# Feed-forward gates in pairs of weight tiles, by seven products of quarters

## The chip, the cores and the metric

The kernel runs on one core of one Trainium2 chip. The time is device microseconds of one execution. The engines are named as in the profile: PE (TensorE, matrix products; PEld is its weight load), DVE (VectorE), ACT (ScalarE), POOL (GpSimd) and SP (SyncE, which issues the DMAs).

## What is computed

One encoder layer on 512 tokens of width 1024: a half-step feed-forward, a mixing stage (gated linear attention and a short convolution), cross-attention to a memory of 256 tokens, a second half-step feed-forward, and a last norm. The change touches the two feed-forwards alone:

```python
def rms_norm(x, g):
    xf = x.astype(jnp.float32)
    y = xf * lax.rsqrt(jnp.mean(xf * xf, axis=-1, keepdims=True) + EPS)
    return (y * g.astype(jnp.float32)).astype(x.dtype)

def swiglu(h, w_gate, w_up, w_down):
    return (jax.nn.silu(h @ w_gate) * (h @ w_up)) @ w_down

x = x + 0.5 * swiglu(rms_norm(x, ffn1_norm[l]), ffn1_w_gate[l], ffn1_w_up[l], ffn1_w_down[l])
...
x = x + 0.5 * swiglu(rms_norm(x, ffn2_norm[l]), ffn2_w_gate[l], ffn2_w_up[l], ffn2_w_down[l])
```

All inputs are fp32; the inner width is 2816.

## The kernel before

Everything lies transposed: 128 channels on the partitions, T = 512 tokens along the free axis. The width 1024 is KD = 8 tiles of 128 rows, the inner width KF = 22 tiles. An fp32 product is made of three products of a reduced type (fp32r): each operand is split into a high part, rounded, and a low part, the rest, and `mm3` (L76 to L79) adds high by high, high by low of x, and low by high. A tile of 128 output channels over the whole width is a "unit": 8 k-tiles by 3 matmuls of 128x512, 24 matmuls into one bank of PSUM.

`unit` (L57) fetches the weights of one unit, 128x1024, by one DMA on SP's queue into `raw` (4 buffers); ACT makes the high part `whi` and DVE the low part `wlo` (`wsplit`, L70 to L72; 3 buffers each). These three steps get a higher priority than their place in the program (AHEAD = 150), and a scheduler then orders each engine's instructions by priority and by which buffers are free. Every engine works through its list in that order.

`ffn` (L237) is called twice, with the name "a" (L360) and "b" (L970). For each of 22 f it computes a gate unit into `pg` and an up unit into `pu`. `finish` (L241) takes both: DVE multiplies them by `rstd`, the norm's factor per token (L243 and L247, into fa and fb), ACT takes silu (L245, fs), POOL multiplies the two into h (L249, fh), and h is split at once into hh (ACT, L126) and hl (DVE, L127), which lie in the pool `big` (44 tiles of 128x512). The norm's gain is in `xs`, the split x; its factor rstd is not needed for the products, and comes only after f = 2 in "a" and f = 1 in "b" (`norm.tok`, `norm.rows`: two matmuls into sp_n and a copy by ACT, L204). After the 22 tiles come 8 tiles d of the output, each with three units of `wd` (DOWN, L235) over the 22 tiles of h.

Four buffers of temporary kinds matter: fa, fb, fs and fh have two buffers each.

Of the kernel before, what the change touches and what calls it, by code (L numbers as in the profile page):

```python
# [20 lines left out]
KF = DFF // P  # L21
# [5 lines left out]
AHEAD = 150  # L27
# [3 lines left out]
def layer_kernel(ctx: ExitStack, tc: tile.TileContext, t: dict, outT: bass.AP):  # L31
    nc = tc.nc
    const = ctx.enter_context(tc.tile_pool(name="const", bufs=1))
    resid = ctx.enter_context(tc.tile_pool(name="resid", bufs=1))
    wpool = ctx.enter_context(tc.tile_pool(name="wpool", bufs=2))
    act = ctx.enter_context(tc.tile_pool(name="act", bufs=1))
    tmp = ctx.enter_context(tc.tile_pool(name="tmp", bufs=2))
# [74 lines left out]
    for i in range(WARM):  # L112
# [4 lines left out]
    gains = const.tile([P, 6, KD], F32, name="gains")  # L117
# [50 lines left out]
    class Norm:  # L168
# [23 lines left out]
        def add(self, d):  # L192
            self.scale(d)
            self.square(d)
# [12 lines left out]
    def first_units(wgu, norm):  # L207

        g, u = unit(None, D, "ga0"), unit(None, D, "ua0")
        sent = []  # L210
        for k in range(0, KD, 2):
            c = slice(k * P, (k + 2) * P)
            queue = nc.scalar if k == 0 else nc.sync
            for n, w in enumerate((g, u)):
                i = queue.dma_start(w[0][:, c], wgu[0, n][:, c])
                if k > 0:
                    sent.append(i)
            if k == 0:
# [12 lines left out]
        norm.scaled = done[-1]  # L231
        return g[1:], u[1:]


    DOWN = ((0, 8), (8, 15), (15, KF))  # L235

    def ffn(wgu, wd, norm, nxt, name, first=None):  # L237
        hs = []
        rstd = None

        def finish(f, pg, pu):  # L241
            a = tmp.tile([P, T], F32, tag="fa", name=f"fa_{name}{f}")
            nc.vector.tensor_tensor(a, pg, rstd, ALU.mult)  # L243
            s = tmp.tile([P, T], F32, tag="fs", name=f"fs_{name}{f}")
            nc.scalar.activation(s, a, AF.Silu)  # L245
            b = tmp.tile([P, T], F32, tag="fb", name=f"fb_{name}{f}")
            nc.vector.tensor_tensor(b, pu, rstd, ALU.mult)  # L247
            h = tmp.tile([P, T], F32, tag="fh", name=f"fh_{name}{f}")
            nc.gpsimd.tensor_tensor(h, s, b, ALU.mult)  # L249
            hh, hl = big(f"hh_{name}{f}", F32R), big(f"hl_{name}{f}", F32R)  # L250
            split(h, hh, hl)
            hs.append((hh, hl))

        waiting = []
        wait = 1 if first is None else 2
        for f in range(KF):
            pg, pu = bank(f"pg_{name}{f}"), bank(f"pu_{name}{f}")
            if f == 0 and first is not None:
                g, u = first
                for k in range(KD):  # L260
                    mm_cols(pg, g, xs, [(k, k)], k == 0, k == KD - 1)
                    mm_cols(pu, u, xs, [(k, k)], k == 0, k == KD - 1)
                for d in range(KD):
                    norm.square(d, norm.scaled)
            else:
                if f == wait:
                    norm.tok()
                behind = norm.landed if f == 1 and first is not None else None
                mm_cols(pg, unit(wgu[f, 0], D, f"g{name}{f}", behind), xs, ALL)
                flush()  # L270
                mm_cols(pu, unit(wgu[f, 1], D, f"u{name}{f}", behind), xs, ALL)
                if f == wait:
                    rstd = norm.rows()
            waiting.append((f, pg, pu))
            if rstd is not None:
                for w in waiting:
                    finish(*w)
                waiting = []

        for d in range(KD):  # L280
            us = [unit(wd[d, :, k0 * P:k1 * P], (k1 - k0) * P, f"d{name}{d}{k0}") for k0, k1 in DOWN]
            if nxt is None and d == KD - 1:
                finale(us, hs)
                return
            ps = bank(f"pd_{name}{d}")
            for u, (k0, k1) in zip(us, DOWN):
                mm_cols(ps, u, hs, [(k - k0, k) for k in range(k0, k1)], k0 == 0, k1 == KF)
            nc.vector.scalar_tensor_tensor(x[d], ps, 0.5, x[d], ALU.mult, ALU.add)
            (nxt or nf).add(d)
# [151 lines left out]
    rstd = nmix.rows()  # L441
# [526 lines left out]

    nf = Norm(GFIN, "nf")
    ffn(t["w2gu"], t["w2d"], n2, None, "b")  # L970


# [61 lines left out]
```

## Time and profile before

| | us |
|---|---|
| median of 3 runs | 1102.85 (1102.79 to 1102.97) |
| profiled execution | 1102.6 |
| its span, from the first to the last instruction | 1100.8 |
| PE busy | 1093.7 (99%) |
| DVE busy | 548.8 (50%) |
| ACT busy | 380.8 (35%) |
| POOL busy | 137.0 (12%) |

Busy time is the sum of an engine's instructions, overlaps within the engine counted once. Matmuls are pipelined: what one costs is the distance between the starts of two that follow one another, not the duration shown. Names such as pg_a stand for all tiles of that name in the stage a.

### The profile page before, as it was taken

How to read it: one execution, taken by the hardware profiler on the slowest of the kernel's cores; microseconds unless marked ns; L12 is line 12 of the kernel's file. 1: busy time of each engine (PE TensorE's matmuls, PEld its weight loads, DVE VectorE, ACT ScalarE, POOL GpSimd, SP SyncE). 2: the span in 40 equal slices, each digit the busy share in tenths (PEclk: the TensorE clock that was granted, in tenths of full speed). 3: DMA queues.
4: the chain of work that ended last, by engine and by line, in shares of the span. 5: the costliest groups of instructions: out<-in, count | busy, mean ns of one | idle time of the engine just before them, and what ended most of it. 6: DMA issues, size and time to landing. Idle time of an engine off the chain costs nothing.

```text
span 1100.8 us, 13905 instructions
## 1 busy us (share of the span) xinstructions
PE 1093.7 (99%) x5736; PEld 918.7 (83%) x5736; DVE 548.8 (50%) x711; ACT 380.8 (35%) x533; POOL 137.0 (12%) x112
## 2 busy tenths in 40 slices
PE   9999999999999999999999999999999999999997
PEld 8888888888888988889888888888888888888887
DVE  6545454543333479776555365635545454532223
ACT  6332223332322364424343344434222222232321
POOL 0211010100111013101002200222101010101000
PEclk9999999999999999999999999999999999999999
DMA  8232323233334322223353221222322323233312
GB/s 265 81 102 92 112 83 110 92 92 90 105 89 123 124 77 92 86 64 130 112 175 96 96 77 39 81 97 92 96 98 94 100 93 110 78 103 99 92 53 78
DMA packets 35136, 109.15 MB, mean 99 GB/s; under 512 B 4992, under 2 KB 8064, under 8 KB 35072
## 3 DMA queue, kind: packets, MB, share of 16 engines
q1 hardware_dynamic: 34640, 107.97, 31.1%
q8 instruction: 45, 0.74, 0.3%
q10 hardware_dynamic: 432, 0.29, 0.1%
q14 instruction: 19, 0.16, 0.0%
HBM read 106.14 MB, written 2.10 MB: 98 GB/s over the span
## 4 chain that ended last, share of the span: by engine, by line
PE 99%; DVE 0%; DVEq 0%; issue 0%; POOL 0%; POOLq 0%
PE pg_a L77 4%; PE pg_b L77 4%; PE pu_a L77 4%; PE pg_a L78 4%; PE pg_a L79 4%; PE pg_b L79 4%; PE pd_a L78 4%; PE pu_b L79 4%; PE pu_a L78 4%; PE pd_a L77 4%; PE pu_a L79 4%; PE pg_b L78 4%; PE pu_b L78 4%; PE pu_b L77 4%; PE pd_a L79 4%; PE pd_b L78 3%
## 5 line engine op out<-in xcount | busy, mean ns | idle before, releaser
L77 PE MATMUL pg_a<-xh,whi_ga 128*128 128x512 f32 x176 | 69.2, 393 | 0.0
L77 PE MATMUL pg_b<-xh,whi_gb 128*128 128x512 f32 x176 | 68.9, 391 | 0.0
L77 PE MATMUL pu_a<-xh,whi_ua 128*128 128x512 f32 x176 | 68.8, 391 | 0.0
L79 PE MATMUL pg_a<-xh,wlo_ga 128*128 128x512 f32 x176 | 68.6, 390 | 0.0
L78 PE MATMUL pg_a<-xl,whi_ga 128*128 128x512 f32 x176 | 68.5, 389 | 0.0
L78 PE MATMUL pg_b<-xl,whi_gb 128*128 128x512 f32 x176 | 68.5, 389 | 0.0
L79 PE MATMUL pg_b<-xh,wlo_gb 128*128 128x512 f32 x176 | 68.5, 389 | 0.0
L79 PE MATMUL pu_b<-xh,wlo_ub 128*128 128x512 f32 x176 | 68.5, 389 | 0.0
L78 PE MATMUL pu_a<-xl,whi_ua 128*128 128x512 f32 x176 | 68.5, 389 | 0.0
L79 PE MATMUL pd_a<-hh_a,wlo_da 128*128 128x512 f32 x176 | 68.5, 389 | 0.0
L79 PE MATMUL pu_a<-xh,wlo_ua 128*128 128x512 f32 x176 | 68.5, 389 | 0.0
L78 PE MATMUL pu_b<-xl,whi_ub 128*128 128x512 f32 x176 | 68.5, 389 | 0.0
L77 PE MATMUL pu_b<-xh,whi_ub 128*128 128x512 f32 x176 | 68.5, 389 | 0.0
L78 PE MATMUL pd_a<-hl_a,whi_da 128*128 128x512 f32 x176 | 68.5, 389 | 0.0
L77 PE MATMUL pd_a<-hh_a,whi_da 128*128 128x512 f32 x176 | 68.5, 389 | 0.0
L78 PE MATMUL pd_b<-hl_b,whi_db 128*128 128x512 f32 x154 | 59.9, 389 | 0.0
L79 PE MATMUL pd_b<-hh_b,wlo_db 128*128 128x512 f32 x154 | 59.9, 389 | 0.0
L77 PE MATMUL pd_b<-hh_b,whi_db 128*128 128x512 f32 x154 | 59.9, 389 | 0.0
L72 DVE TENSOR_TENSOR wlo_db<-raw_db,whi_db 128x896 fp32r<-128x896 f32 (+1 forms) x24 | 28.4, 1182 | 53.8 <-ACT whi_db L71 53.1
L249 POOL TENSOR_TENSOR fh_a<-fs_a,fb_a 128x512 f32<-128x512 f32 x22 | 31.9, 1452 | 185.3 <-DVE fb_a L247 154.5
L249 POOL TENSOR_TENSOR fh_b<-fs_b,fb_b 128x512 f32<-128x512 f32 x22 | 30.4, 1381 | 197.8 <-DVE fb_b L247 171.5
L72 DVE TENSOR_TENSOR wlo_da<-raw_da,whi_da 128x896 fp32r<-128x896 f32 (+1 forms) x24 | 28.4, 1182 | 49.8 <-ACT whi_da L71 49.1
(351 smaller groups left out, 2651.2 us busy)
## 6 DMA issues: line engine op xcount, KB each, us to landing
raw_gb<-in_w2gu SPq DMA_DIRECT2D x22, 512.0 KB, 3.5
raw_ub<-in_w2gu SPq DMA_DIRECT2D x22, 512.0 KB, 3.4
raw_ga<-in_w1gu SPq DMA_DIRECT2D x21, 512.0 KB, 3.5
raw_ua<-in_w1gu SPq DMA_DIRECT2D x21, 512.0 KB, 3.4
raw_da<-in_w1d SPq DMA_DIRECT2D x16, 448.0 KB, 3.4
raw_db<-in_w2d SPq DMA_DIRECT2D x16, 448.0 KB, 3.3
raw_da<-in_w1d SPq DMA_DIRECT2D x8, 512.0 KB, 3.6
raw_wk<-in_wk SPq DMA_DIRECT2D x8, 512.0 KB, 3.7
```

The lines of the kernel that those rows point to most:

```text
L72: nc.vector.tensor_tensor(lo[:, c], raw[:, c], hi[:, c].bitcast(F32), ALU.subtract))
L77: nc.tensor.matmul(ps, lhsT=whi, rhs=xhi, start=start, stop=False)
L78: nc.tensor.matmul(ps, lhsT=whi, rhs=xlo, start=False, stop=False)
L79: last_mm[0] = nc.tensor.matmul(ps, lhsT=wlo, rhs=xhi, start=False, stop=stop)
L249: nc.gpsimd.tensor_tensor(h, s, b, ALU.mult)
```

## The change

The gate tiles f and f+1 are computed as a pair, for f = 4, 6, ... 18 in "a" and f = 2, 4, ... 18 in "b" (8 and 9 pairs); f = 20 and 21 and the first tiles stay as they were, and so do all up units. The pair is one product of a 2 by 2 block matrix of weights (two tiles by two halves of the width) with a 2 by 2 block matrix of x (two halves of the width by two halves of the tokens). It is done by Strassen's scheme in Winograd's form: seven products of quarters instead of eight, each 4 k-tiles by 3 matmuls of 128x256, 84 matmuls of 256 columns (`seventh`) in place of 48 of 512. Four combinations of the halves of the weights are made in place in the two raw tiles, per pair (`pair_units`): four DVE instructions of 512 columns (L294, L302, L303, L312), and seven 512-column splits on ACT and DVE (L282, L283) into four tiles W0 to W3. Four combinations of the quarters of x are made once per stage (`quarter_sums`, `fill` of k = 0 to 3; L248 to L257), with their splits, into 16 tiles of `big` called t0 to t3. The results are summed up after the products: U is a copy by ACT (L353), the other five sums are DVE instructions of 128x256 that read PSUM (`add`, L350).

The 16 tiles take room in `big`. So h of f below 15 stays one fp32 tile, and is split later, at f = 20 and 21 (`late`).

PE's order in a pair, by the products' names: A (first half, with W0), Dq (W0), nine matmuls of the up unit, B (W1), three of the up unit, A (second half, W1), the rest of the up unit, B (W2), seven of the second up unit, Fq (W2), the rest of it, Dq (W3).

```diff
+    def quarter_sums(gi, name):
+        tiles = [[big(f"t{n}_{name}{k}", F32R) for k in range(KD // 2)] for n in range(4)]
+        def fill(k):
+            b1 = tmp.tile([P, T], F32, tag="fb", name=f"b1_{name}{k}")
+            b2 = tmp.tile([P, T], F32, tag="fs", name=f"b2_{name}{k}")
+            nc.scalar.activation(b1, x[k], AF.Copy, scale=gains[:, gi, k:k + 1])
+            nc.scalar.activation(b2, x[k + 4], AF.Copy, scale=gains[:, gi, k + 4:k + 5])
+            e, l = slice(0, HALF_T), slice(HALF_T, T)
+            ta = tmp.tile([P, T], F32, tag="fa", name=f"ta_{name}{k}")
+            tb = tmp.tile([P, T], F32, tag="fh", name=f"tb_{name}{k}")
+            sums = (tb[:, l], tb[:, e], ta[:, e], ta[:, l])
+            nc.vector.tensor_tensor(sums[2], b1[:, l], b1[:, e], ALU.subtract)
+            nc.vector.tensor_tensor(sums[1], b2[:, l], sums[2], ALU.subtract)
+            nc.vector.tensor_tensor(sums[0], b2[:, l], b1[:, l], ALU.subtract)
+            nc.vector.tensor_tensor(sums[3], b2[:, e], sums[1], ALU.subtract)
+            for n in range(4):
+                split(sums[n], tiles[n][k][:, e], tiles[n][k][:, l])
+        return tiles, fill
...
+        FIRST, LAST = (4 if first is not None else 2), 20
+        KEPT = 15
...
+            def halves(raw, c, hi, lo, at):
+                nc.scalar.activation(hi[:, at], raw[:, c], AF.Copy)
+                nc.vector.tensor_tensor(lo[:, at], raw[:, c], hi[:, at].bitcast(F32), ALU.subtract)
...
+                    halves(a, q0, *w, q0)
+                    nc.vector.tensor_tensor(a[:, q0], a[:, q0], b[:, q0], ALU.subtract)
+                    halves(a, q0, *w, q1)
...
+                    nc.vector.tensor_tensor(b[:, q0], b[:, q0], b[:, q1], ALU.add)
+                    nc.vector.tensor_tensor(a[:, q0], b[:, q1], a[:, q0], ALU.subtract)
+                    halves(a, q0, *w, q0)
+                    halves(a, q1, *w, q1)
...
+                    nc.vector.tensor_tensor(a[:, q1], a[:, q1], a[:, q0], ALU.subtract)
+                    halves(b, q0, *w, q0)
+                    halves(a, q1, *w, q1)
...
+                    halves(b, q1, *w, q0)
...
+        def seventh(ps, w, at, xb, start):
+            for k in range(KD // 2):
+                c = slice(at + k * P, at + (k + 1) * P)
+                for n, (wq, xq) in enumerate(((w[0], xb[k][0]), (w[0], xb[k][1]), (w[1], xb[k][0]))):
+                    nc.tensor.matmul(ps, lhsT=wq[:, c], rhs=xq, start=(start and k == 0 and n == 0),
+                                     stop=(k == KD // 2 - 1 and n == 2), skip_group_check=True)
...
+        def pair(f):
...
+            A, B, Dq, Fq = ab[:, e], ab[:, l], df[:, e], df[:, l]
...
+            U, V, E, C12 = c2[:, l], c2[:, e], c1, c1
...
+            seventh(A, w, 0, xq(0, e), True)
+            nc.scalar.copy(U, A)
+            seventh(Dq, w, T, t3, True)
+            w = units[1]()
+            seventh(B, w, 0, t2, False)
+            add(V, U, B)
+            seventh(A, w, T, xq(4, e), False)
+            mm_cols(pus[0], unit(wgu[f, 1], D, f"u{name}{f}"), xs, ALL)
+            w = units[2]()
+            seventh(B, w, 0, t1, False)
+            add(E, U, B)
+            add(c2[:, l], E, Dq)
+            seventh(Fq, w, T, xq(4, l), False)
+            add(C12, E, Fq)
+            finish(f, ((A, e), (C12, l)), pus[0])
+            mm_cols(pus[1], unit(wgu[f + 1, 1], D, f"u{name}{f + 1}"), xs, ALL)
+            w = units[3]()
+            seventh(Dq, w, 0, t4, False)
+            add(c2[:, e], V, Dq)
+            finish(f + 1, ((c2, slice(0, T)),), pus[1])
...
+            if f < KEPT:
+                h = big(f"h_{name}{f}")
+            else:
+                h = tmp.tile([P, T], F32, tag="fh", name=f"fh_{name}{f}")
...
+            if f < KEPT:
+                late.append(two)
+            else:
+                two()
...
+            if FIRST <= f < LAST:
+                if (f - FIRST) % 2 == 0:
+                    pair(f)
+                continue
...
+            if f >= LAST:
+                for _ in range(len(late) // (KF - f)):
+                    late.pop(0)()
...
+            if f < FIRST and (first is None or f > 0):
+                for _ in range(-(-len(fills) // (FIRST - f))):
+                    fills.pop(0)()
```

How it moves instructions is shown at three places. In the rows, the number behind the stage's letter is f, the last number is the program's own count. On DVE, from the products of tile 4 with rstd on, the order before is:

```order
L243 TENSOR_TENSOR fa_a4_574<-pg_a4_512,rstd_n1_400 128x512
L72 TENSOR_TENSOR wlo_ua5_620<-raw_ua5_618,whi_ua5_619 128x1024
L247 TENSOR_TENSOR fb_a4_578<-pu_a4_513,rstd_n1_400 128x512
L72 TENSOR_TENSOR wlo_ga6_664<-raw_ga6_662,whi_ga6_663 128x1024
L127 TENSOR_TENSOR hl_a4_583<-fh_a4_580,hh_a4_582 128x512
L243 TENSOR_TENSOR fa_a5_648<-pg_a5_586,rstd_n1_400 128x512
L72 TENSOR_TENSOR wlo_ua6_694<-raw_ua6_692,whi_ua6_693 128x1024
```

Each unit's low part stands between two instructions that wait for PE. After the change, from the last product of Fq on (the first row is the later half of tile 4; c1 is C12, the sum that reads Fq, c2 holds U, V and the results of tile 5), DVE has this order; raw_ga6 and raw_ga7 are the tiles a and b of the next pair:

```order
L376 TENSOR_TENSOR fa_a4_723<-c1_a4_588,rstd_n1_452 128x256
L283 TENSOR_TENSOR wlo_g0a6_798<-raw_ga6_793,whi_g0a6_797 128x512
L294 TENSOR_TENSOR raw_ga6_793<-raw_ga6_793,raw_ga7_795 128x512
L302 TENSOR_TENSOR raw_ga7_795<-raw_ga7_795 128x512
L283 TENSOR_TENSOR wlo_g0a6_798<-raw_ga6_793,whi_g0a6_797 128x512
L303 TENSOR_TENSOR raw_ga6_793<-raw_ga7_795,raw_ga6_793 128x512
L380 TENSOR_TENSOR fb_a5_783<-pu_a5_587,rstd_n1_452 128x512
L283 TENSOR_TENSOR wlo_g1a6_830<-raw_ga6_793,whi_g1a6_829 128x512 x2
L312 TENSOR_TENSOR raw_ga6_793<-raw_ga6_793 128x512
L72 TENSOR_TENSOR wlo_ua6_864<-raw_ua6_862,whi_ua6_863 128x1024
L350 TENSOR_TENSOR c2_a4_589<-c2_a4_589,pdf_a4_585 128x256
L376 TENSOR_TENSOR fa_a5_779<-c2_a4_589,rstd_n1_452 128x512
```

The two weight tiles W0 and W1 of the next pair and its first up unit now stand together, between the sum that waits for Fq and the last sum of the pair. On ACT the same stretch before is:

```order
L245 ACTIVATE fs_a4_576<-fa_a4_574 128x512
L71 ACTIVATE whi_ga6_663<-raw_ga6_662 128x1024
L126 ACTIVATE hh_a4_582<-fh_a4_580 128x512
L71 ACTIVATE whi_ua6_693<-raw_ua6_692 128x1024
L245 ACTIVATE fs_a5_650<-fa_a5_648 128x512
```

And after, from silu of tile 4 on:

```order
L378 ACTIVATE fs_a4_726<-fa_a4_723 128x512
L282 ACTIVATE whi_g0a6_797<-raw_ga6_793 128x512
L282 ACTIVATE whi_g1a6_829<-raw_ga6_793 128x512 x2
L71 ACTIVATE whi_ua6_863<-raw_ua6_862 128x1024
L282 ACTIVATE whi_g2a6_892<-raw_ga7_795 128x512
L282 ACTIVATE whi_g2a6_892<-raw_ga6_793 128x512
L378 ACTIVATE fs_a5_781<-fa_a5_779 128x512
L353 COPY c2_a6_792<-pab_a6_787 128x256
```

The copy U of the next pair (last row) stands behind silu of tile 5, which reads fa of tile 5, the last row of DVE's list above. The third place is DVE ahead of the first pair of "a". Before:

```order
L243 TENSOR_TENSOR fa_a3_500<-pg_a3_438,rstd_n1_400 128x512
L72 TENSOR_TENSOR wlo_ua4_546<-raw_ua4_544,whi_ua4_545 128x1024
L127 TENSOR_TENSOR hl_a2_435<-fh_a2_432,hh_a2_434 128x512
L247 TENSOR_TENSOR fb_a3_504<-pu_a3_439,rstd_n1_400 128x512
L72 TENSOR_TENSOR wlo_ga5_590<-raw_ga5_588,whi_ga5_589 128x1024
```

After, from fb of tile 3 on:

```order
L380 TENSOR_TENSOR fb_a3_562<-pu_a3_497,rstd_n1_452 128x512
L72 TENSOR_TENSOR wlo_ua4_661<-raw_ua4_659,whi_ua4_660 128x1024
L127 TENSOR_TENSOR t3_a2_198<-ta_a2_482,t3_a2_198 128x256
L254 TENSOR_TENSOR ta_a3_570<-b1_a3_566 128x256
L256 TENSOR_TENSOR tb_a3_571<-b2_a3_567,b1_a3_566 128x256
L255 TENSOR_TENSOR tb_a3_571<-b2_a3_567,ta_a3_570 128x256
L257 TENSOR_TENSOR ta_a3_570<-b2_a3_567,tb_a3_571 128x256
L127 TENSOR_TENSOR t0_a3_187<-tb_a3_571,t0_a3_187 128x256
L127 TENSOR_TENSOR t1_a3_191<-tb_a3_571,t1_a3_191 128x256
```

The up unit's low part (L72) stands behind the two products of tile 3 and most of the fill of k = 2, and the fill of k = 3 stands behind that.

## Rows read from the trace of the kernel before

**Rows 1.** The page: busy time by engine, granted clock by slice, the chain
```profile
PE 1093.7 (99%) x5736; PEld 918.7 (83%) x5736; DVE 548.8 (50%) x711; ACT 380.8 (35%) x533; POOL 137.0 (12%) x112
...
PEclk9999999999999999999999999999999999999999
...
PE 99%; DVE 0%; DVEq 0%; issue 0%; POOL 0%; POOLq 0%
```

**Rows 2.** PE's timeline: start, duration, line, out<-in, shape; 24 matmuls apart
```profile
61.86 0.39 PE L77 MATMUL pg_a<-xh,whi_ga 128*128 128x512 f32 x1
...
67.30 0.39 PE L77 MATMUL pu_a<-xh,whi_ua 128*128 128x512 f32 x1
```

**Rows 3.** PE's timeline, 256 columns: the first and the fifty-first
```profile
507.00 0.28 PE L77 MATMUL mkps<-mem,whi_wk 128*128 128x256 f32 x1
...
513.00 0.28 PE L79 MATMUL mkps<-mem,wlo_wk 128*128 128x256 f32 x1
```

**Rows 4.** DVE's groups by shape: count | busy us, mean ns | idle before
```profile
L72 DVE TENSOR_TENSOR wlo_ua<-raw_ua,whi_ua 128x1024 fp32r<-128x1024 f32 x21 | 25.7, 1224 | 4.5 <-ACT whi_ua L71 4.5
...
L243 DVE TENSOR_TENSOR fa_a<-pg_a,rstd_n 128x512 f32<-128x512 f32 x22 | 15.2, 690 | 26.5 <-PE pg_a L79 26.5
...
L750 DVE TENSOR_TENSOR mk<-mkps,mk 128x256 fp32r<-128x256 f32 x8 | 3.3, 418 | 0.0
```

**Rows 5.** DVE's timeline: two independent instructions in a row
```profile
43.02 0.68 DVE L243 TENSOR_TENSOR fa_a<-pg_a,rstd_n 128x512 f32<-128x512 f32 x1
43.62 0.68 DVE L247 TENSOR_TENSOR fb_a<-pu_a,rstd_n 128x512 f32<-128x512 f32 x1
```

**Rows 6.** DVE and POOL at three places: timelines of either engine, x counts merged ones
```profile
106.50 2.32 DVE L72 TENSOR_TENSOR wlo_ga<-raw_ga,whi_ga 128x1024 fp32r<-128x1024 f32 x1 [0.23 <-ACT whi_ga L71]
...
106.44 1.29 POOL L249 TENSOR_TENSOR fh_a<-fs_a,fb_a 128x512 f32<-128x512 f32 x1 [9.59 <-DVE fb_a L247]
...
410.05 1.77 DVE L517 TENSOR_TENSOR mn<-k,mn 128x512 f32<-128x512 f32 x1
...
408.99 2.29 POOL L519 TENSOR_TENSOR ta<-k,ta 128x512 f32<-128x512 f32 x1
...
430.54 2.26 DVE L568 SCALAR_TENSOR_TENSOR S<-S,dec,dS 128x128 f32<-128x128 f32 x6
...
430.77 1.29 POOL L709 TENSOR_TENSOR cv<-cv,rstd_nmix 128x512 f32<-128x512 f32 x1 [13.62 <-DVE cv L708]
```

**Rows 7.** ACT's groups by shape: silu
```profile
L245 ACT ACTIVATE fs_a<-fa_a 128x512 f32<-128x512 f32 x22 | 13.5, 616 | 1.7 <-DVE fa_a L243 1.7
```

**Rows 8.** Timelines of ACT and PE in stage a: rstd, and the first matmul of f = 4
```profile
40.56 0.57 ACT L204 COPY rstd_n<-sp_n 128x512 f32<-128x512 f32 x1
...
50.98 0.39 PE L77 MATMUL pg_a<-xh,whi_ga 128*128 128x512 f32 x1
```

**Rows 9.** Stage b: first matmul of f = 2 (PE), table load, DVE's first product, POOL's h
```profile
751.25 0.40 PE L77 MATMUL pg_b<-xh,whi_gb 128*128 128x512 f32 x1
...
752.32 1.28 ACT L245 ACT_TABLE_LOAD   x1
...
753.00 0.68 DVE L243 TENSOR_TENSOR fa_b<-pg_b,rstd_n 128x512 f32<-128x512 f32 x1
...
754.43 2.54 POOL L249 TENSOR_TENSOR fh_b<-fs_b,fb_b 128x512 f32<-128x512 f32 x2 [10.47 <-ACT fs_b L245]
```

**Rows 10.** DMA issues: out<-in, queue, count, KB each, median us to landing
```profile
raw_ga<-in_w1gu SPq DMA_DIRECT2D x21, 512.0 KB, 3.5
```

More of the change, by code (lines that the diff above doesn't have):

```diff
@@ L235, in layer_kernel @@
     DOWN = ((0, 8), (8, 15), (15, KF))
+    HALF_T = T // 2
+    def quarter_sums(gi, name):
[16 more added lines that the diff above has]
+        return tiles, fill
@@ L237, in ffn, with pair_units, tiles, first_two @@
     def ffn(wgu, wd, norm, nxt, name, first=None):
-        hs = []
+        hs = [None] * KF
         rstd = None
+        FIRST, LAST = (4 if first is not None else 2), 20
+        KEPT = 15
+        tq, fill = quarter_sums(norm.gi, name)
+        late = []
+        def pair_units(f):
+            q0, q1 = slice(0, T), slice(T, D)
+            raws = []
+            def tiles(n, m):
+                return (wpool.tile([P, m], F32R, tag="whi", name=f"whi_g{n}{name}{f}", bufs=3),
+                        wpool.tile([P, m], F32R, tag="wlo", name=f"wlo_g{n}{name}{f}", bufs=3))
+            def halves(raw, c, hi, lo, at):
+                nc.scalar.activation(hi[:, at], raw[:, c], AF.Copy)
+                nc.vector.tensor_tensor(lo[:, at], raw[:, c], hi[:, at].bitcast(F32), ALU.subtract)
+            def first_two():
+                with tc.high_priority(AHEAD):
+                    for i in range(2):
+                        raw = wpool.tile([P, D], F32, tag="raw", name=f"raw_g{name}{f + i}", bufs=4)
+                        nc.sync.dma_start(raw, wgu[f + i, 0])
+                        raws.append(raw)
+                    a, b = raws
+                    w = tiles(0, D)
+                    halves(a, q0, *w, q0)
+                    nc.vector.tensor_tensor(a[:, q0], a[:, q0], b[:, q0], ALU.subtract)
+                    halves(a, q0, *w, q1)
+                return w
+            def next_two():
+                with tc.high_priority(AHEAD):
+                    a, b = raws
+                    w = tiles(1, D)
+                    nc.vector.tensor_tensor(b[:, q0], b[:, q0], b[:, q1], ALU.add)
+                    nc.vector.tensor_tensor(a[:, q0], b[:, q1], a[:, q0], ALU.subtract)
+                    halves(a, q0, *w, q0)
+                    halves(a, q1, *w, q1)
+                return w
+            def third_two():
+                with tc.high_priority(AHEAD):
+                    a, b = raws
+                    w = tiles(2, D)
+                    nc.vector.tensor_tensor(a[:, q1], a[:, q1], a[:, q0], ALU.subtract)
+                    halves(b, q0, *w, q0)
+                    halves(a, q1, *w, q1)
+                return w
+            def final_one():
+                with tc.high_priority(AHEAD):
+                    a, b = raws
+                    w = tiles(3, D)
+                    halves(b, q1, *w, q0)
+                return w
+            return first_two, next_two, third_two, final_one
@@ new lines, in seventh, with xq @@
+        def seventh(ps, w, at, xb, start):
[4 more added lines that the diff above has]
+                                     stop=(k == KD // 2 - 1 and n == 2), skip_group_check=True)
+                tick()
+        def pair(f):
+            e, l = slice(0, HALF_T), slice(HALF_T, T)
+            def xq(k0, tok):
+                return [(xs[k0 + k][0][:, tok], xs[k0 + k][1][:, tok]) for k in range(KD // 2)]
+            t3, t2, t1, t4 = [[(q[:, e], q[:, l]) for q in row] for row in tq]
+            units = pair_units(f)
+            ab, df = bank(f"pab_{name}{f}"), bank(f"pdf_{name}{f}")
+            pus = [bank(f"pu_{name}{f + i}") for i in range(2)]
+            A, B, Dq, Fq = ab[:, e], ab[:, l], df[:, e], df[:, l]
+            c1 = tmp.tile([P, T], F32, tag="sq", name=f"c1_{name}{f}", bufs=2)[:, 0:HALF_T]
+            c2 = tmp.tile([P, T], F32, tag="c2", name=f"c2_{name}{f}", bufs=1)
+            U, V, E, C12 = c2[:, l], c2[:, e], c1, c1
+            add = lambda o, a, b: nc.vector.tensor_tensor(o, a, b, ALU.add)
+            w = units[0]()
+            seventh(A, w, 0, xq(0, e), True)
[18 more added lines that the diff above has]
+            finish(f + 1, ((c2, slice(0, T)),), pus[1])
@@ L241, in finish @@
         def finish(f, pg, pu):
             a = tmp.tile([P, T], F32, tag="fa", name=f"fa_{name}{f}")
-            nc.vector.tensor_tensor(a, pg, rstd, ALU.mult)
+            for part, tok in pg:
+                nc.vector.tensor_tensor(a[:, tok], part, rstd[:, tok], ALU.mult)
             s = tmp.tile([P, T], F32, tag="fs", name=f"fs_{name}{f}")
@@ L247, in finish, with two @@
             nc.vector.tensor_tensor(b, pu, rstd, ALU.mult)
-            h = tmp.tile([P, T], F32, tag="fh", name=f"fh_{name}{f}")
+            if f < KEPT:
+                h = big(f"h_{name}{f}")
+            else:
+                h = tmp.tile([P, T], F32, tag="fh", name=f"fh_{name}{f}")
             nc.gpsimd.tensor_tensor(h, s, b, ALU.mult)
-            hh, hl = big(f"hh_{name}{f}", F32R), big(f"hl_{name}{f}", F32R)
-            split(h, hh, hl)
-            hs.append((hh, hl))
+            def two():
+                hs[f] = big(f"hh_{name}{f}", F32R), big(f"hl_{name}{f}", F32R)
+                split(h, *hs[f])
+            if f < KEPT:
+                late.append(two)
+            else:
+                two()
         waiting = []
         wait = 1 if first is None else 2
+        fills = [lambda k=k: fill(k) for k in range(KD // 2)]
         for f in range(KF):
+            if FIRST <= f < LAST:
+                if (f - FIRST) % 2 == 0:
+                    pair(f)
+                continue
             pg, pu = bank(f"pg_{name}{f}"), bank(f"pu_{name}{f}")
@@ L273, in ffn @@
                     rstd = norm.rows()
-            waiting.append((f, pg, pu))
+            if f >= LAST:
+                for _ in range(len(late) // (KF - f)):
+                    late.pop(0)()
+            waiting.append((f, ((pg, slice(0, T)),), pu))
             if rstd is not None:
@@ L278, in ffn @@
                 waiting = []
+            if f < FIRST and (first is None or f > 0):
+                for _ in range(-(-len(fills) // (FIRST - f))):
+                    fills.pop(0)()
+        for two in late:
+            two()
         for d in range(KD):
```

## The prediction

> **What bounds the kernel now.** I read the page's first parts, then PE's timeline, then the other engines in the stretches that the change touches. PE is busy for 1093.7 of 1100.8 us, the chain that ended last is 99% PE and the granted clock reads 9 in every slice, while DVE is busy half of the time and POOL an eighth [rows 1]. So time is lost or won only where PE has fewer columns to stream or has to wait. Two things about PE's price must be seen. A 128x512 matmul occupies its slot for 0.2267 us: the first of a gate unit starts at 61.86 and the first of the next unit, 24 matmuls on, at 67.30 [rows 2]; the 0.39 us in the duration column is the length of one in the pipeline. A 128x256 matmul that changes its weights each time occupies 0.1200 us: fifty of them lie between 507.00 and 513.00 [rows 3]. Half the columns cost 53% of the slot.
>
> **What PE gains.** Two gate units were 48 matmuls of 512 columns: 48 x 0.2267 = 10.88 us. Seven products of 12 matmuls of 256 columns are 84 x 0.1200 = 10.08 us. A pair gains 0.80 us, and 8 pairs in the first stage ("a", f from 4 to 19) and 9 in the second ("b", f from 2) gain 13.6 us if PE never waits. A pair with its two up units then has 20.96 us of PE work against 21.76 before. The gain is thin: it is gone if a 256-column matmul takes 10.88/84 = 129.5 ns.
>
> The Trainium skill ("TensorE: Matmul & The Clock Gate", section "Back-to-back issue gap") gives sustained spacings of 81 ns for 128 and 131 ns for 512 columns, so that few columns are dear; about 98 ns for 256 by a straight line would make seven products 8.2 us against 6.3 and the change a loss of 1.9 us a pair. The trace does not agree: its spacings for this data type are 120 and 226.7 ns [rows 2, 3], and the sum goes by them.
>
> **What DVE gets.** Prices: 1024 columns 1.22, 512 columns 0.69, 256 columns 0.42 us from start to end [rows 4]; an instruction that depends on nothing just before it starts 0.60 us after a 512 one [rows 5]. Per pair of f, DVE had four splits of 1024 (L72), two of 512 (L127) and four products with rstd, some 9 us in 21.76. Now it has two 1024, fourteen 512 and seven 256, about 2 x 1.15 + 14 x 0.65 + 7 x 0.4 = 14 to 15 us in 20.96. That fits in the sum. It does not fit in the order: the sums of PE's results stand in DVE's one queue ahead of the next pair's weights, so DVE can't begin on most of the next weights until the seventh product of this pair but one (Fq) is out.
>
> I set zero at the start of a pair's first product. By PE's order the slots end: A first half 1.44, Dq 2.88, three quarters of a unit of up in pieces around B and A's second half until 11.20, B 12.64, Fq 15.67, second up unit 19.52, Dq 20.96; in the next pair A and Dq again to 23.84, then nine up matmuls to 25.88, then B. B writes the bank that ACT's copy U (L353) reads, so its first matmul waits for U. U stands on ACT behind silu of f+1, which waits for fa of f+1, which stands on DVE behind the whole preparation. The queue from Fq, each end in us: C12 16.30 (a 256-column result in PSUM is readable some 0.2 after its slot), fa's later half 16.73, W0 low part 17.34, a-=b 18.05, then POOL (next paragraph) and b+= 19.77, W0's second low part 20.38, a=b-a 21.09, fb 21.69, two low parts of W1 22.90, a-=a 23.50, the up unit's low part (1024) 24.65, c2's earlier half 24.98, fa 25.69; ACT then has silu (0.62 [rows 7]) to 26.34 and U to 26.61. B could start at 25.88 and starts at 26.66: **0.77 us of waiting per step from pair to pair**, of which the up unit's low part, wanted at 24.29 by its third matmul and ready at 24.65, is already 0.36. One pair then takes about 21.73 us, against 21.76 before: the gain is given back.
>
> **POOL inside that queue.** h of f (L385, two SBUF inputs) is released by its silu near 17.4 and asks while DVE runs a-=b. The trace shows how two such instructions meet: POOL's product alone takes 1.29; started at 106.44, it made DVE's split of 106.50 take 2.32 instead of 1.23; in the stretch at 409 the two engines take turns, POOL's instruction at 408.99 lasting 2.29 and DVE's at 410.05 lasting 1.77 instead of 0.69. DVE instructions that read PSUM are not held: six from 430.54 took 2.26, 0.377 each, while POOL ran from 430.77 [rows 6]. So b+= waits for POOL, about 1.1 us. Lower bound of this term: zero, if POOL is the one that waits; upper: 1.2. I take 1.1, by the rows at 106 and 410. Before, the same collision cost nothing, because PE's next weights were two units ahead.
>
> The Trainium skill ("VectorE: DVE Perf Modes", section "The DRAIN you can't avoid") says that the next DVE instruction does not start until the pipe is empty. Rows at 43.02 and 43.62 show a 0.69 us instruction overlapped by 0.09 [rows 5]; by that rule seven or eight independent instructions of the queue would cost 0.6 us more per pair, some 9 us in all. The trace decides, and the sum has the overlap.
>
> Of 15 steps from pair to pair 13 are of this kind: 13 x 0.77 = 10.0 us. In the other two (16 to 18 in each stage) an h that is not kept is split at once, one more 512 instruction on each of DVE and ACT ahead of the up unit: 0.77 + 0.6 = 1.4 each, 2.8 us. Bounds for a step are 0 (POOL waits) and 1.4.
>
> **Start of the pairs.** The sums of x (fill) of k = 2 and 3 stand behind rstd. In "a" rstd ends at 41.13 and the pair's first product would start at 50.98 [rows 8]. DVE's queue from there holds 15 instructions of 512, seven of 256 and one of 1024 up to the up unit's low part: 9.0 + 2.6 + 1.2 = 12.8 us, and POOL takes two to three turns for h0, h1, h2: it ends near 56.5. The third up matmul wants it at 53.93: 2.6 us. The fill of k = 3 (one low part, four sums, two more low parts and POOL's h3) follows to 59.8, and PE, which has gone on to 58.5, waits 1.3 more: **3.9 us**. In "b" the pair would start at 751.25; rstd is followed by a table load of 1.28 us, and DVE's first product starts at 753.00 [rows 9]. The buffers for the fills come free only after POOL's h0 and h1, which end at 756.97 in the trace [rows 9]; the fill of k = 3 is ready at 763.6 and the next up unit's high part, for which a buffer of W0 must come free, at 764.6, where PE by its own work would be at 761.0: **3.6 us**. Bounds for the two together: 4 (no turns of POOL) and 9.
>
> **What costs nothing.** ACT (U, silu, copies) has some 11 us in a pair. Post-sums V and c2's later half are ready within 0.2 us of need. The same bytes are loaded; b's raw tile is freed at 12.7, and a load lands in 3.5 us [rows 10], at 16.2, 1.1 us before a-=b wants it. Late splits: 15 h of 1.3 us on DVE and ACT, some 20 us, lie in the two plain gate and up units (21.8 us) and the first down unit, whose matmuls want h one after another. If that cover is gone the cost is 1 or 2 us per stage.
>
> **Sum.** -13.6 + 10.0 + 2.8 + 3.9 + 3.6 = +6.7 us, on a profiled execution of 1102.6 us (span 1100.8) beside a median of 1102.85. Forecast 1109.5 us.
>
> **Rivals.**
> - PE stays the bound: POOL waits for DVE's run of back-to-back instructions instead of breaking in, 1.1 us leaves the queue, and a step costs nothing (25.88 against 25.5). Then -13.6 + 2 x 0.3 + 7 = -6: 1097 us, **faster**. For it: POOL's instruction of 408.99 did wait for DVE. Against: it then got its turn. It decides from 0.8 us of queue less per pair.
> - A draw: the collision is half as dear or falls later. A step of 0.4: -13.6 + 6 + 7 = -0.6: 1102 us.
> - A longer queue: every DVE instruction pays its whole duration (0.6 us a step), b's tile lands late, V or c2 is late too: 1.5 per step: -13.6 + 22.5 + 8.5 = +17: 1120 us.
> - The narrow products don't run at 0.120: at 0.1295 the gain is nil and the waits stay small, since PE is slower: about 1110. It moves no end of the range. Against it: fifty in a row at 0.1200 [rows 3].
>
> **How the numbers follow.** About 0.2% (2.2 us) is what a measurement of this kernel can tell from no change. Forecast 0.50 (its own range 1104 to 1116), faster rival 0.25, draw 0.15, longer queue 0.07, narrow products 0.03. Faster by over 0.2%: 0.25 and a fifth of the draw, 0.28. Slower: nearly all of the forecast, the longer queue and the narrow products, 0.56. Within 0.2%: 0.16. Both signs hold much of the chance, so the range runs from 1094 (faster rival with starts of 4 us) to 1118.
>
> **What the profile would show.** Right: in the pairs PE's B waits on ACT's copy of A, 0.5 to 1.1 us each time, the pair takes 21.5 to 22.0 us, a DVE sum on the raw tiles lasts near 1.8 instead of 0.69 beside POOL's h, and PE idles some 4 us soon after each rstd. Wrong: pairs of 20.96 us with no wait, or products at a spacing other than 0.120.

## The result: 17.8 us slower, mainly through queues

| | before | after |
|---|---|---|
| median of 4 runs each, us | 1102.85 | 1120.61 (1120.01 to 1121.47) |
| ratio to before, 95% interval | 1 | 1.0161 (1.0144 to 1.0179) |
| profiled execution's span, us | 1100.8 | 1119.8 |

The direction was forecast, the size was not: +6.7 us was worked out, +17.8 came, and 1120.6 lies above the range (1118). The page of the changed kernel, against [rows 1]: PE's matmuls are busy for 4 us more although they stream fewer columns (busy time counts durations: of the 0.60 us between two starts below, 0.40 count as busy), DVE for 107 us more, and the granted clock's row shows 9 throughout, since a slice of 28 us hides what a few us show.

```profile
PE 1097.4 (98%) x6348; PEld 934.3 (83%) x6348; DVE 656.1 (59%) x1030; ACT 440.4 (39%) x683; POOL 148.7 (13%) x112
...
PEclk9999999999999999999999999999999999999999
```

The time from one pair's first matmul to the next pair's, read from PE's timeline, shows where the 19.0 us between the spans lie. Each pair took 21.76 before (two f), and 84 x 0.1200 + 48 x 0.2267 = 20.96 is PE's work now. One usual step, from PE's timeline:

```profile
99.41 0.28 PE L331 MATMUL pab_a<-xh,whi_g0a 128*128 128x256 f32 x1
...
121.53 0.28 PE L331 MATMUL pab_a<-xh,whi_g0a 128*128 128x256 f32 x1
```

All steps:

| stretch | stage a | stage b |
|---|---|---|
| first pair | 24.89 | 26.46 |
| steps to f = 6 ... 14 (a), 4 ... 14 (b) | 22.05 to 22.12 | 22.27, then 22.09 to 22.11 |
| f = 16 | 22.92 | 22.93 |
| f = 18 (to the first matmul of f = 20) | 23.50 | 23.50 |

Over 20.96, that is 3.9 + 5.5 us in the first pairs, 12.7 in eleven usual steps and 9.0 in four last ones. The pairs of "a" also begin 1.5 late (52.47 for 50.98). With the 13.6 that the columns save: -13.6 + 3.9 + 5.5 + 12.7 + 9.0 + 1.5 = 19.0. The rest of the kernel, the two stretches with the late splits among it, takes what it took (the two plain tiles 21.8 us in either stage).

One usual step as PE's timeline has it (start, duration, line, out<-in, shape; in brackets its idle time just before and what ended it). Two rows that follow one another, 0.23 apart where nothing is in the way:

```profile
102.52 0.40 PE L78 MATMUL pu_a<-xl,whi_ua 128*128 128x512 f32 x1
103.12 0.50 PE L79 MATMUL pu_a<-xh,wlo_ua 128*128 128x512 f32 x1 [0.20 <-DVE wlo_ua L72]
103.46 0.40 PE L77 MATMUL pu_a<-xh,whi_ua 128*128 128x512 f32 x1
...
104.60 0.39 PE L79 MATMUL pu_a<-xh,wlo_ua 128*128 128x512 f32 x1
105.17 0.50 PE L331 MATMUL pab_a<-t_a,whi_g1a 128*128 128x256 f32 x2 [0.17 <-ACT c_a L353]
```

PE stands for 0.60 instead of 0.23 before the up unit's third matmul, the first that needs its low part, and for 0.57 before B, which waits for ACT's copy U: 0.37 and 0.34. Behind each wait the second start is late too: 103.46 lies 0.34 behind 103.12. So the nine up matmuls up to B take 2.88 instead of 2.04, 0.84 more. The queue behind it, in ACT's timeline (silu of f+1, then U) and in DVE's (the tile combinations; the low part of the up unit; fa of f+1), and POOL's product:

```profile
104.22 0.63 ACT L378 ACTIVATE fs_a<-fa_a 128x512 f32<-128x512 f32 x1 [0.65 <-DVE fa_a L376]
104.76 0.35 ACT L353 COPY c_a<-pab_a 128x256 f32<-128x256 f32 x1
```

```profile
95.81 0.69 DVE L294 TENSOR_TENSOR raw_ga<-raw_ga,raw_ga 128x512 f32<-128x512 f32 x1
96.54 1.66 DVE L302 TENSOR_TENSOR raw_ga<-raw_ga 128x512 f32<-128x512 f32 x1
...
101.85 1.22 DVE L72 TENSOR_TENSOR wlo_ua<-raw_ua,whi_ua 128x1024 fp32r<-128x1024 f32 x1
102.99 0.42 DVE L350 TENSOR_TENSOR c_a<-c_a,pdf_a 128x256 f32<-128x256 f32 x1
103.44 0.69 DVE L376 TENSOR_TENSOR fa_a<-c_a,rstd_n 128x512 f32<-128x512 f32 x1
...
95.98 1.67 POOL L385 TENSOR_TENSOR h_a<-fs_a,fb_a 128x512 f32<-128x512 f32 x1 [11.54 <-ACT fs_a L378]
```

POOL's instruction starts at 95.98, while L294 runs, and by its length gets its turn near that one's end; b+= (L302) takes 1.66 instead of 0.69. That is [rows 6] again, with 0.97 us. The Trainium skill, "SBUF — State Buffer", section "SBUF: two separate sides", tells of one pair of ports for DVE and GpSimd, taken whole by a GpSimd instruction or by a DVE instruction with two SBUF inputs, whichever starts first, while the other waits; the 1.66 and the 1.67 here agree.

### The profile page after: what moved, and what is told of

Read it like the earlier page. It is cut to its first block, busy times and chain, and to the rows that moved or that the text cites. A ratio compares the mean times of both kernels' runs of the same rounds, so it can differ in the third digit from the quotient of the medians.

```text
span 1119.8 us, 15728 instructions
## 1 busy us (share of the span) xinstructions
PE 1097.4 (98%) x6348; PEld 934.3 (83%) x6348; DVE 656.1 (59%) x1030; ACT 440.4 (39%) x683; POOL 148.7 (13%) x112
## 5 line engine op out<-in xcount | busy, mean ns | idle before, releaser
L72 DVE TENSOR_TENSOR wlo_db<-raw_db,whi_db 128x896 fp32r<-128x896 f32 (+1 forms) x24 | 27.3, 1136 | 52.1 <-ACT whi_db L71 51.6
L72 DVE TENSOR_TENSOR wlo_da<-raw_da,whi_da 128x896 fp32r<-128x896 f32 (+1 forms) x24 | 27.3, 1136 | 48.1 <-ACT whi_da L71 47.6
L71 ACT ACTIVATE whi_da<-raw_da 128x896 fp32r<-128x896 f32 (+1 forms) x24 | 23.7, 987 | 72.2 <-PE pd_a L78 52.5
L71 ACT ACTIVATE whi_db<-raw_db 128x896 fp32r<-128x896 f32 (+1 forms) x24 | 23.7, 988 | 70.6 <-PE pd_b L78 52.5
L72 DVE TENSOR_TENSOR wlo_ub<-raw_ub,whi_ub 128x1024 fp32r<-128x1024 f32 x22 | 26.9, 1222 | 30.1 <-ACT whi_ub L71 30.1
L79 PEld LDWEIGHTS pu_a<-xh,wlo_ua 128*128 128x128 f32 x176 | 33.1, 188 | 12.8 <-DVE wlo_ua L72 6.3
L79 PEld LDWEIGHTS pu_b<-xh,wlo_ub 128*128 128x128 f32 x176 | 33.1, 188 | 11.9 <-DVE wlo_ub L72 5.5
L385 POOL TENSOR_TENSOR h_a<-fs_a,fb_a 128x512 f32<-128x512 f32 x15 | 25.8, 1722 | 126.0 <-ACT fs_a L378 107.8
L385 POOL TENSOR_TENSOR h_b<-fs_b,fb_b 128x512 f32<-128x512 f32 x15 | 23.7, 1582 | 140.7 <-ACT fs_b L378 140.7
L72 DVE TENSOR_TENSOR wlo_ua<-raw_ua,whi_ua 128x1024 fp32r<-128x1024 f32 (+1 forms) x25 | 27.3, 1093 | 22.3 <-ACT whi_ua L71 22.3
```

## Experiments

Each kernel is the changed one with the edit shown (the last one: the kernel before). Times are medians, beside runs of the kernel before on the same chip (1102.8 for the first four, 1103.1 for the others).

### POOL's product left out

```diff
-            nc.gpsimd.tensor_tensor(h, s, b, ALU.mult)
+            paired = FIRST <= f < LAST
+            s = h if paired else tmp.tile([P, T], F32, tag="fs", name=f"fs_{name}{f}")
...
+            if not paired:
+                nc.gpsimd.tensor_tensor(h, s, b, ALU.mult)
```

> In the pairs h is silu alone: POOL's product of silu and up is left out there (the up units, their product with rstd and all else stay). Theory (DVE's one queue from Fq to the next pair's copy U sets the step, and POOL's product breaks into it for 1.0 us): a pair's period falls from 22.10 to about 21.1, the steps at f=16 and 18 from 22.9 and 23.5 to about 22, the starts of the stages stay. Sum about -15 us, 1105 to 1107. Rival (POOL's product is harmless, the length of DVE's queue alone or the changes between 256 and 512 columns on PE cost the time): -4 us at most, period 21.8 or more.

Measured: 1104.98 us, ratio to before 1.0021 (1.0012 to 1.0030), 15.6 less than the change. The usual step took 21.33 to 21.42, those of f = 16 and 18 21.27 to 21.49 (about 22 was expected), the first pairs 24.90 and 26.66. Two first matmuls of pairs (PE's timeline), and b+=, which is back at its own length (DVE's):

```profile
97.56 0.28 PE L331 MATMUL pab_a<-xh,whi_g0a 128*128 128x256 f32 x1
...
118.92 0.28 PE L331 MATMUL pab_a<-xh,whi_g0a 128*128 128x256 f32 x1
```

```profile
93.97 0.69 DVE L294 TENSOR_TENSOR raw_ga<-raw_ga,raw_ga 128x512 f32<-128x512 f32 x1
94.69 0.69 DVE L302 TENSOR_TENSOR raw_ga<-raw_ga 128x512 f32<-128x512 f32 x1
```

So POOL's products, on an engine that is busy for 13% of the span, carry 15.6 of the 17.8 us. By the steps some 8.5 of them lie in the eleven usual ones, where one product holds DVE for 0.97 us, and 7.4 in the four last ones, where the splits of h wait for the products as well. The usual step fell by 0.77, less than the 0.97 and less than the 1.0 expected: only 0.84 lay in the stretch up to B, and 0.07 of it stays. In all 0.38 us over 20.96 stay, with no wait of PE's named in that step. The first pairs did not fall.

### The copy U ahead of silu

```diff
-            c1 = tmp.tile([P, T], F32, tag="sq", name=f"c1_{name}{f}", bufs=2)[:, 0:HALF_T]
+            c1 = tmp.tile([P, T], F32, tag="sq", name=f"c1_{name}{f}", bufs=2)
...
-            U, V, E, C12 = c2[:, l], c2[:, e], c1, c1
+            U, V, E, C12 = c1[:, l], c2[:, e], c1[:, e], c1[:, e]
...
-            nc.scalar.copy(U, A)
+            with tc.high_priority(AHEAD):
+                nc.scalar.copy(U, A)
```

> The copy U gets half a tile of its own (the unused half of c1) and stands on ACT ahead of silu of f+1. Theory: B no longer waits for U, which is 0.3 to 0.4 us of each step; the up unit's low part is still 0.37 late and V as late as now. Period from 22.10 to about 21.75; sum -4 to -6 us, 1115 to 1117. Rival (B waits for the low part of W1, or U for its buffer only): no change of the period, 1120.

Measured: 1116.09 us, ratio 1.0120 (1.0105 to 1.0135), 4.5 less. The sum came as expected, the reason did not. The usual step took 21.96 to 22.03, only 0.1 less. B now follows Dq with no wait, but the scheduler put B ahead of the up unit, and the next in line was late at once: A's second half waits for V (L350), which stands on DVE behind the same queue (PE's timeline; 1.06 between the two starts):

```profile
104.07 0.40 PE L78 MATMUL pu_a<-xl,whi_ua 128*128 128x512 f32 x1
105.13 0.39 PE L331 MATMUL pab_a<-xh,whi_g1a 128*128 128x256 f32 x1 [0.67 <-DVE c_a L350]
```

Most of what was gained lies in f = 16 and 18, which fell to 21.99 and 22.11 with the new order. The wait moved: the length of DVE's queue sets the step, whichever of its users is last.

### Pairs begin two tiles later

```diff
-        FIRST, LAST = (4 if first is not None else 2), 20
+        FIRST, LAST = (6 if first is not None else 4), 20
```

> The first pair is two tiles later in either stage (f=6 in a, f=4 in b), so one pair fewer in each. Theory (at the start of the pairs PE waits for the sums of x of k=2 and 3, which stand in DVE's queue behind rstd): the first pairs, now 24.9 and 26.5, fall to the usual 22.1, and two pairs fewer change the rest by less than 1 us: -7 to -8 us, about 1113. Rival (the fills are tied to the first pair and come as late again): the first pairs stay at 24 or more, 1118 to 1121.

Measured: 1112.80 us, ratio 1.0090 (1.0075 to 1.0105), 7.8 less. The first pairs took 21.24 and 22.46. The sums of x were there in time, but for one wait of 1.2 us in "b". The granted clock did not fall in either start, as it did in "b" of the changed kernel (below). So 7.8 us is the price of the two starts, with the clock's part and some 0.7 us for two usual steps fewer.

### All h of the pairs kept

```diff
-        KEPT = 15
+        KEPT = 20
```

> All h of the pairs are kept in fp32 and split at f=20 and 21 (KEPT 20 instead of 15). Theory (the steps of f=16 and 18 are longer than the others, 22.9 and 23.5 against 22.1, because splits of h stand ahead of V and of the up unit's low part on DVE): these steps fall to 22.1, -4 to -5 us; five more splits on DVE and ACT at f=20 and 21 of each stage cost nothing while PE has 21.8 us there. 1115 to 1117. Rival (these steps are longer because tiles of the pool come free late, or the late splits then hold the down units): no gain, or a loss of 1 to 4 us.

Measured: 1117.96 us (1116.27 to 1119.96), ratio 1.0138 (1.0122 to 1.0155), 2.7 less. The steps of f = 16 and 18 fell to 22.08 to 22.11, the usual step, which is 4.4 us in all. The profiled run gave some of it back in the first pairs, 25.47 and 27.94, where the edit changes nothing but the clock fell for longer (below). The late splits, five more in each stage, cost nothing: the two plain tiles took 21.8 us.

### The product on DVE, behind V

```diff
+            def product(behind):
+                i = nc.vector.tensor_tensor(h, s, b, ALU.mult)
+                if behind is not None:
+                    after(i, behind)
+
+            if FIRST <= f < LAST:
+                owed.append(product)
+            else:
+                nc.gpsimd.tensor_tensor(h, s, b, ALU.mult)
...
-            add(V, U, B)
+            pay(add(V, U, B))
```

`pay` issues the two products that the pair before owes, ordered behind V on DVE.

> The product of silu and up of a pair is done by DVE instead of POOL, behind the sum V of the next pair (of the last pair at f=20); the output is the full one. Theory (POOL's product breaks into DVE's queue where it is tight; DVE has idle time after V): the pair's period falls from 22.10 to about 21.35, as in the run without that product, though DVE does 1.3 us more per pair; steps at f=16 and 18 to 21.5 to 22; sum -14 to -16 us, 1104 to 1107. Rival (DVE is short of time as such, and a product is dear wherever it stands): period 22.1 or more, 1120 or slower.

Measured: 1105.35 us, ratio 1.0021 (1.0011 to 1.0030). The steps took 21.33 to 21.35, f = 16 and 18 included; only the one behind the first pair of "b" took 21.54. Two first matmuls of pairs:

```profile
97.81 0.28 PE L336 MATMUL pab_a<-xh,whi_g0a 128*128 128x256 f32 x1
...
119.14 0.28 PE L336 MATMUL pab_a<-xh,whi_g0a 128*128 128x256 f32 x1
```

DVE does more work than before the edit and the kernel is 15 us faster: DVE's total was never the bound.

### Four edits together, and three of them

The first has U ahead of silu, the product on DVE, KEPT = 20 and the later start.

> Four changes together: U ahead of silu, product by DVE behind V, all h of the pairs split at f=20 and 21, pairs from f=6 and f=4. Theory (the waits at the start, at the steps and at the last steps are separate, and what is left is PE's own 21.34 us a pair): 15 pairs at 0.42 us below the 21.76 of before, some 1 us of waits at the starts: 1097 to 1099, faster than before by 4 to 6 us. Rival (taking one wait away uncovers another, as with U alone): periods of 21.7 or more, 1103 or slower.

Measured: 1095.16 us, ratio 0.9928 (0.9915 to 0.9942): 8.0 us below the kernel before. The usual step is 21.05 to 21.07, 0.3 below what was expected: with U ahead of silu B follows Dq directly. Two first matmuls of pairs that follow one another, and all that PE waited for in the whole span (total, times, longest):

```profile
117.87 0.28 PE L336 MATMUL pab_a<-xh,whi_g0a 128*128 128x256 f32 x1
...
138.94 0.28 PE L336 MATMUL pab_a<-xh,whi_g0a 128*128 128x256 f32 x1
```

```profile
PE pu_a L77 <- ACT whi_ua L71: 1.3, 1, 1.3
PE pdf_b L336 <- ACT t_b L126: 1.2, 1, 1.2
PE warm L113 <- POOL mhalf L107: 1.1, 1, 1.1
```

On DVE the products (L393) stand in what was idle time, with V just ahead of them:

```profile
122.80 0.42 DVE L355 TENSOR_TENSOR c_a<-c_a,pab_a 128x256 f32<-128x256 f32 x1
123.13 1.29 DVE L393 TENSOR_TENSOR h_a<-fs_a,fb_a 128x512 f32<-128x512 f32 x2
126.03 1.23 DVE L72 TENSOR_TENSOR wlo_ua<-raw_ua,whi_ua 128x1024 fp32r<-128x1024 f32 x1 [1.61 <-ACT whi_ua L71]
```

The second has the first three edits, with the pairs from f = 4 and 2.

> The same without the later start: pairs from f=4 and f=2. Theory: all steps at 21.3 to 21.4, the first pairs still 25 and 27: 1104 to 1106, some 7 us above the run with the later start, which shows the price of the two starts by itself. Rival: the starts too were long because of POOL's products, and fall with them: 1100 or less.

Measured: 1102.38 us, ratio 0.9991 (0.9982 to 1.0000), 7 above the run with the later start. It cannot be told from the kernel before. The steps are the same 21.05 to 21.13; the first pairs take 24.90 and 27.71. Some 3 of the 7 us are the granted clock, as far as one execution tells: the one with a mean of 0.999 took 1099.22, the other nine, with 0.994 to 0.997, took 1101.21 to 1103.78. The rival for the starts (POOL's products) is out: they belong to the sums of x, not to the pairs' products.

### The kernel before, with gate units in halves

```diff
-                mm_cols(pg, unit(wgu[f, 0], D, f"g{name}{f}", behind), xs, ALL)
+                for i in range(2):
+                    tok = slice(i * T // 2, (i + 1) * T // 2)
...
+                            nc.tensor.matmul(pg[:, tok], lhsT=wq[:, c], rhs=xq[:, tok], ...)
```

> The kernel before, but with 43 of its 44 gate units done in two halves of 256 tokens (48 matmuls of 256 columns instead of 24 of 512), nothing else changed. It measures the narrow matmul and the change between widths without DVE's queue. By 0.1200 and 0.2267 us: 43 x 0.32 = 13.7 us, 1116.6. Theory (a change of width costs PE 0.03 to 0.09 us each time): 2 to 5 us more, 1118 to 1122. Rival (the change of width is free, the 0.38 us a pair left without POOL's product are small waits): 1116 to 1117.

Measured: 1118.13 us, ratio 1.0137 (1.0123 to 1.0151), +15.0, of which 13.7 are 43 x 0.32 by the prices of [rows 2, 3]. Of the remaining 1.3 us the rows show 0.02 a unit, 0.9 in all (PE's timeline; the gate unit from 64.72 to 70.48 takes 48 x 0.1200 to the digit, the up unit from 70.48 to 75.94 takes 5.46 for 5.44); the rest is not placed:

```profile
64.72 0.28 PE L275 MATMUL pg_a<-xh,whi_ga 128*128 128x256 f32 x1
...
70.48 0.40 PE L77 MATMUL pu_a<-xh,whi_ua 128*128 128x512 f32 x1
...
75.94 0.28 PE L275 MATMUL pg_a<-xh,whi_ga 128*128 128x256 f32 x1
```

So the price of the narrow matmul holds also where nothing is late, and a change of width costs about 0.02 to 0.03, just below the 0.03 to 0.09 that were expected. The 0.10 over 20.96 in a pair of the fastest kernel is four such changes.

## Why the prediction was wrong in size

The forecast was +6.7 us, and the spans differ by 19.0. Three terms of the sum failed and make up most of the 12.3 between them: the eleven usual steps at 1.15 instead of 0.77 (4.2), the four last ones at 9.0 us together instead of 4.3 (4.7) and the start of "b" at 5.5 instead of 3.6 (1.9). The other 1.5 lie ahead of the pairs and stood in no term.

- **What PE gains: right.** 0.1200 per narrow matmul, in the pairs too (12 from 121.53 in the changed kernel take 1.44), so -13.6 us. The figures of the Trainium skill that the prediction quotes ("TensorE: Matmul & The Clock Gate", section "Back-to-back issue gap"), by which the products would have been dearer by themselves, don't hold for these matmuls.
- **POOL inside the queue: right.** 1.1 us were taken, 0.97 measured; without it the step loses 0.77, just the amount forecast. POOL waits a little as well (1.67 us for 1.29), but the rival in which it alone waits is out by the 1.66 us of b+=.
- **The usual step: mechanism right, size short.** The waits for the up unit's low part (0.36 forecast, 0.37 measured) and then for U (0.41 and 0.34) are there as worked out. The queue too ran by its forecast: counted from the end of Fq's last slot (94.10 in the step above), the up unit's low part was out after 8.97 us (8.98 forecast) and fa of f+1 after 10.03 (10.02). The stretch up to B costs 0.84, of which 0.07 remains without POOL's product. What was missing is 0.38 a step, 1.15 instead of 0.77, of which 0.31 lies outside that stretch. The sum had it at zero: PE's row was taken as 84 slots and 48 slots laid end to end. Parts of it are changes of width, 0.02 to 0.03 each. The greater part, some 0.25, lies around the two products with W1, and went when B followed Dq directly (21.34 to 21.07). In the run without POOL's product either one begins late and its first two matmuls start 0.22 apart instead of 0.12, the distance seen elsewhere behind a wait. So waits too short to be listed are likely; no run told it apart. The second of them (PE's timeline):

```profile
125.91 0.39 PE L79 MATMUL pu_a<-xh,wlo_ua 128*128 128x512 f32 x1
126.18 0.38 PE L331 MATMUL pab_a<-xh,whi_g1a 128*128 128x256 f32 x1
126.40 0.28 PE L331 MATMUL pab_a<-xl,whi_g1a 128*128 128x256 f32 x1
126.52 0.28 PE L331 MATMUL pab_a<-xh,wlo_g1a 128*128 128x256 f32 x1
```

- **The last steps: the term most wrong.** Two were counted, at 1.4 each; there are four, of 2.0 and 2.5 (9.0 us instead of 4.3, which is 2.8 for the two and 1.5 for two counted as usual ones). The step named was "16 to 18 in each stage ... one more 512 instruction". In truth h of f = 15 is split within the pair f = 16, and there the split (L127) stands ahead of V; h of f = 16 and 17 within the pair f = 18, the first ahead of the up unit's low part, the second ahead of V. The timelines of ACT and DVE in the pair f = 16, where the split waits for ACT, which waits for POOL's product, and V (L350) follows:

```profile
194.95 0.63 ACT L126 ACTIVATE hh_a<-fh_a 128x512 fp32r<-128x512 f32 x1 [1.40 <-POOL fh_a L385]
...
195.62 0.69 DVE L127 TENSOR_TENSOR hl_a<-fh_a,hh_a 128x512 fp32r<-128x512 f32 x1 [1.85 <-ACT hh_a L126]
196.22 0.41 DVE L350 TENSOR_TENSOR c_a<-c_a,pab_a 128x256 f32<-128x256 f32 x1
```

  V starts 2.62 us behind B's first matmul (193.60), in the usual step 1.78 (106.95 behind 105.17): 0.84 late, and this step is 0.81 longer than the usual one. I priced the split by its own 0.6 us and not by what it waits for with V behind it. Keeping all h takes these steps back to the usual one.
- **The starts: "a" right, "b" short.** 3.9 forecast and 3.9 measured in "a". In "b" 3.6 became 5.5, of which the waits are some 4.1 and the clock 1.4. While PE was busy for 0.89 and then 1.31 of 2 us, the granted clock fell to 0.5, which is 1.2 GHz, and the pair ran on (stretch, length, busy us of PE, PEld, DVE, ACT and POOL with counts, then the clock, and the DMA engines' share and GB/s):

```profile
771.00:773.00 2.00, 0.89 (x3) 0.57 (x4) 2.00 (x7) 1.23 (x4) 0.00 (x0) 1.00 0.21 25
773.00:775.00 2.00, 1.31 (x6) 0.97 (x6) 1.79 (x5) 1.06 (x1) 0.00 (x0) 0.70 0.66 238
775.00:777.00 2.00, 2.00 (x11) 2.00 (x10) 1.14 (x2) 0.00 (x0) 0.00 (x0) 0.50 0.25 27
777.00:779.00 2.00, 2.00 (x17) 1.99 (x16) 0.70 (x2) 0.63 (x1) 0.00 (x0) 0.95 0.61 236
```

  11 matmuls instead of the 16 or 17 that these 2 us would hold at full clock; the stretches bound the loss at 0.6 + 1.0 + 0.1 = 1.7 us. PE's timeline gives the 1.4, which is an estimate: from the first row below the up matmul takes 0.59 instead of 0.23, and the product of 12 up to the third 2.45 instead of 1.44. No run has this start without the fall.

```profile
774.33 0.80 PE L77 MATMUL pu_b<-xh,whi_ub 128*128 128x512 f32 x1 [0.69 <-ACT whi_ub L71]
774.92 0.42 PE L331 MATMUL pab_b<-xh,whi_g1b 128*128 128x256 f32 x1
...
777.37 0.40 PE L331 MATMUL pab_b<-t_b,whi_g2b 128*128 128x256 f32 x2
```

- **Ahead of the pairs.** 1.5 us in "a" were in no term. 0.8 of them lie before the first matmul of f = 0 (6.13 instead of 5.34, an ACT wait for a load; that matmul starts at 5.3 to 6.1 in the runs here). The other 0.7 lie between 14.9 and 19.1, behind another load, for which ACT waits 0.93 us up to 13.82. The fills of k = 0 and 1 stand on ACT and DVE among the first splits, but they are not the cause: in four of five other runs with the same fills (no product on POOL, U early, all h kept, product on DVE) the first pair follows the first matmul of f = 0 after 45.6 to 45.9 us, as before (45.6), against 46.3 here; the fifth, three edits together, took 47.2 with a wait of 1.3 us for ACT at its start. So the 1.5 are mostly of the single execution, and much of why the spans differ by 19.0 and the medians by 17.8.
- **What was costed at nothing.** The late splits were hidden, as said, and so were the loads of b. V "within 0.2 us of need" was right for the usual step, wrong where a split stood ahead of it.
- **The rival with the nearest number.** "A longer queue" named 1120 us, and 1120.6 came, but that is luck. Its 1.5 in every step was to come from instructions that pay their whole duration, late tiles of b and a late V. Instructions still overlapped (101.85 and 102.99 on DVE lie 1.14 apart for 1.22), b's tiles were in time, V was late in the four last steps alone, and the usual step cost 1.15.
- **The rule on DVE.** The section of the Trainium skill that the prediction quotes for it ("VectorE: DVE Perf Modes", "The DRAIN you can't avoid") itself excepts an instruction that is not held, which starts earlier. So the overlap of [rows 5] does not speak against that page.

The range failed because its upper end took one bound after another from single instructions (1.4 for the dearest step) and gave the longer queue 0.07. Most of its unknowns lean to the same side: each adds to one queue.

## What to carry to other kernels

A change that trades the bounding engine's time for work on an idle one is paid for in order, not in sum: look which results stand behind the new work in the idle engine's queue, and what is released into the middle of it from other engines. A step with three users of one queue is not mended at one of them; in the usual step U ahead of silu alone gave 0.1 us, taking the intruder out of the queue (POOL's 0.97 us) 0.77, and the place for its work was the same engine's idle time two waits later. And where a step of a schedule is unlike the others, price it from its own order: the four odd steps cost as much as eight of the usual ones.

## What the runs showed of the hardware

- A 512-column matmul behind a 256-column one costs 0.02 to 0.03 us more than in its own kind's company (5.46 for 5.44 a unit); a 256-column one behind a 512-column one nothing (5.76 for 48).
- Behind a wait PE's second start is late as well, by 0.10 to 0.11 us (103.12 and 103.46: 0.34 for 0.23; 126.18 and 126.40 where only a short wait can be: 0.22 for 0.12).
- The granted clock fell to half in "b" at 773.8, where PE had work but matmuls started up to 1.25 us apart (771.55 to 772.80); in "a" of the same execution starts up to 1.08 apart left it at full. With all h kept, which leaves the starts as they were, it fell in "a" as well and for twice as long in "b": the first pairs took 25.47 and 27.94 instead of 24.89 and 26.46. So the price of the starts varies by some 2 us from run to run with the same instructions. The Trainium skill, "TensorE: Matmul & The Clock Gate", section "HAM oscillation — how this bites in real kernels", describes such a fall where PE waits for a load between groups of matmuls. The rows agree in that PE idled before the fall; here it stood for 0.86 us at most at a time.
- A POOL product of two SBUF inputs that meets a running DVE instruction of the same kind waits for its end and then holds up the next one (1.67 and 1.66 us for 1.29 and 0.69 alone).
